# Two blocks on one core: common runs of transposes, and modulation products in 16 runs

## The chip, the cores and the metric

The kernel runs on one core of a Trainium2 chip. The metric is its time on the device in microseconds (us). The core has TensorE (PE; its weight loads are shown as PEld), VectorE (DVE), ScalarE (ACT), GpSimd (POOL) and SyncE (SP), whose queue issues the loads from memory.

## What is computed

Two residual blocks, one behind the other, each of two layers, on 256 tokens of width 1024. A layer of the first block multiplies the tokens by a wide weight matrix, runs three kinds of attention on the parts, gates the result, multiplies by an output matrix and normalizes. A layer of the second block normalizes its 256 tokens and 256 context tokens, scales and shifts them by a modulation that comes from two vectors, multiplies by `w_in`, runs a convolution, a gated linear attention and a softmax attention, merges them under gates, and adds the result, scaled by the modulation's third part:

```python
shift_x, scale_x, gate_x = jnp.split(jax.nn.silu(c) @ w_mod + b_mod, 3, axis=-1)
shift_c, scale_c, gate_c = jnp.split(jax.nn.silu(c_ctx) @ w_mod + b_mod, 3, axis=-1)
hx = rms_norm(xs, norm_g) * (1 + scale_x[:, None]) + shift_x[:, None]
...
xs = xs + gate_x[:, None] * merge(px, ya_x, yb_x, yc_x)
```

All of it is in float32.

## The kernel before

**Weights.** Every product of tokens and weights is made of three matmuls (`mm3`, lines 183 to 186): weights and tokens are each split into a rounded high part (`wh`, made by ScalarE) and a rest (`wl`, made by VectorE). They are called split matmuls here. `WStream` (line 111) holds one table of all weight entries, 512 KB each for the most part, in the order of their use. `_dma` loads the next entry into one of four buffers (`wraw`), `_split` splits it into one of five pairs of buffers (`wh`, `wl`), and `get(key)` first brings loads and splits ahead by so many entries of the table (6 and 3 for most of the kernel) and then hands out the parts of `key`. A `wraw` buffer comes free when its entry is split. All loads go through SP's queue in the table's order.

**Modulation.** `w_mod` is 48 more entries (units) of the same table, 24 for each layer of block 2, in three sets of eight for shift, scale and gate. They are not split. `mod_stream` (line 762) takes one unit, multiplies it with the two vectors (line 770: four products with 32 columns of weights each, side by side in the array, 8 instructions in the trace), and yields; behind the eighth unit of a set it copies the sums, turns them by four small matmuls (line 778) and adds the bias. A unit's `wraw` buffer comes free when its products are done. `FILL` (line 42) says before the use of which weights how many units are taken: 24 places, 24 units in the second layer of block 1, 16 in the first of block 2, 8 in its second. A unit stands in the table just ahead of the weights before which it is used, and counts as an entry of the look-ahead.

**Transposes.** Between the gemms, tokens-by-features results are turned by matmuls with the identity into one of three PSUM banks (`at`) and copied out. In block 1: `gemm` (line 238) calls `post` for each of the two token blocks, and `post_a` and `post_rope` turn the rotated result (lines 292, 271); `gate` (line 576) turns the gated result (line 581) for the output product `go`; `flip` (line 654) turns rows at the end. In block 2: `post_k` (line 928) turns low-rank gates and keys (lines 938, 952), `scores` (line 1022) turns queries and the negated row maxima (lines 1031, 1053), `weigh` (line 1058) turns the attention's output (line 1091), `conv_finish` (line 1330) turns forth and back (lines 1337, 1349), and `norm_prep` (line 791) sums squares by small matmuls (line 815).

**Order.** The program is written in the order of use; a scheduler then lays down each engine's queue ahead of time, taking what is ready by priority (earlier in the program first, unless `high_priority` says otherwise). On the chip each queue runs in the order laid down. `STEPS` gives the order of block 1's steps: gemms A to I, index scores `ix`, attentions `ds`, `df`, `fo`, and gates `h`, `i`, each for token blocks 0 and 1. `g.wait(a, b)` makes instruction a wait for b.

## Time and profile before

| | |
|---|---|
| median of 3 runs | 1189.15 us (1187.99 to 1195.4) |
| the profiled execution's own time | 1192.62 us |
| its span, first to last instruction | 1190.8 us |
| busy: PE, PEld | 1168.5 us, 975.7 us |
| busy: DVE, ACT, POOL | 921.1 us, 569.5 us, 11.2 us |
| mean granted TensorE clock | 0.999 |

The profile is of one execution. Busy time is the time in which an engine had an instruction in work. Matmuls overlap: one starts before the one ahead of it has ended, so the distance from start to start tells more than an instruction's duration.

### The profile page before, as it was taken

How to read it: one execution, taken by the hardware profiler on the slowest of the kernel's cores; microseconds unless marked ns; L12 is line 12 of the kernel's file. 1: busy time of each engine (PE TensorE's matmuls, PEld its weight loads, DVE VectorE, ACT ScalarE, POOL GpSimd, SP SyncE). 2: the span in 40 equal slices, each digit the busy share in tenths (PEclk: the TensorE clock that was granted, in tenths of full speed). 3: DMA queues.
4: the chain of work that ended last, by engine and by line, in shares of the span. 5: the costliest groups of instructions: out<-in, count | busy, mean ns of one | idle time of the engine just before them, and what ended most of it. 6: DMA issues, size and time to landing. Idle time of an engine off the chain costs nothing.

```text
span 1190.8 us, 20632 instructions
## 1 busy us (share of the span) xinstructions
PE 1168.5 (98%) x8024; PEld 975.7 (82%) x8024; DVE 921.1 (77%) x2051; ACT 569.5 (48%) x1024; POOL 11.2 (1%) x42
## 2 busy tenths in 40 slices
PE   8999999999999999999999999999999999999998
PEld 6788777677887777767887888888999778999998
DVE  6996766967799859989545986755799897896984
ACT  5556634456555433247444422433455534855552
POOL 0000000000000000000000000000000000000000
PEclk9999999999999999999999999999999999999999
DMA  7634566465555642024221232325545333554552
GB/s 263 224 125 127 186 207 225 155 229 195 177 194 181 230 137 89 19 73 145 68 84 59 89 100 78 106 89 177 178 142 186 96 107 123 179 162 127 174 176 72
DMA packets 47538, 171.33 MB, mean 144 GB/s; under 512 B 5260, under 2 KB 5900, under 8 KB 46672
## 3 DMA queue, kind: packets, MB, share of 16 engines
q1 hardware_dynamic: 47440, 170.01, 43.7%
q8 instruction: 63, 1.03, 0.3%
q14 instruction: 35, 0.29, 0.1%
HBM read 167.89 MB, written 2.10 MB: 143 GB/s over the span
## 4 chain that ended last, share of the span: by engine, by line
PE 76%; DVE 11%; DMA 6%; ACT 5%; issue 2%; SPq 0%; ACTq 0%; DVEq 0%
PE f0m L186 3%; PE f0m L185 3%; PE f0m L184 3%; PE f1m L186 2%; PE f1m L184 2%; PE f1m L185 2%; PE po L185 1%; PE po L186 1%; PE po L184 1%; PE mod L770 1%; PE go L186 1%; PE go L185 1%; PE go L184 1%; PE yog L186 1%; PE yoc L186 1%
## 5 line engine op out<-in xcount | busy, mean ns | idle before, releaser
L1012 DVE SCALAR_TENSOR_TENSOR ucv<-up,par,ucv 128x512 f32<-128x512 f32 (+1 forms) x240 | 147.3, 614 | 2.8
L184 PE MATMUL f0m<-hTh,wh_0m 128*128 128x512 f32 x192 | 75.1, 391 | 0.0
L185 PE MATMUL f0m<-hTl,wh_0m 128*128 128x512 f32 x192 | 75.1, 391 | 0.0
L186 PE MATMUL f0m<-hTh,wl_0m 128*128 128x512 f32 x192 | 74.8, 390 | 0.0
L184 PE MATMUL f1m<-hTh,wh_1m 128*128 128x256 f32 x192 | 54.9, 286 | 0.1
L186 PE MATMUL f1m<-hTh,wl_1m 128*128 128x256 f32 x192 | 54.8, 286 | 0.0
L185 PE MATMUL f1m<-hTl,wh_1m 128*128 128x256 f32 x192 | 54.5, 284 | 0.0
L154 ACT CAST wh_0m<-wr_0m 128x1024 fp32r<-128x1024 f32 x24 | 25.1, 1047 | 55.9 <-PE f0m L185 14.5
L155 DVE TENSOR_TENSOR wl_0m<-wr_0m,wh_0m 128x1024 fp32r<-128x1024 f32 x24 | 29.3, 1222 | 18.2 <-ACT wh_0m L154 18.1
L184 PEld LDWEIGHTS f0m<-hTh,wh_0m 128*128 128x128 f32 x192 | 36.1, 188 | 7.4
L185 PEld LDWEIGHTS f0m<-hTl,wh_0m 128*128 128x128 f32 x192 | 36.1, 188 | 7.3
L186 PEld LDWEIGHTS f0m<-hTh,wl_0m 128*128 128x128 f32 x192 | 36.1, 188 | 7.3
L184 PEld LDWEIGHTS f1m<-hTh,wh_1m 128*128 128x128 f32 x192 | 36.8, 191 | 0.5 <-ACT wh_1m L154 0.3
L186 PEld LDWEIGHTS f1m<-hTh,wl_1m 128*128 128x128 f32 x192 | 36.7, 191 | 0.2 <-DVE wl_1m L155 0.2
L185 PEld LDWEIGHTS f1m<-hTl,wh_1m 128*128 128x128 f32 x192 | 36.8, 191 | 0.1
L154 ACT CAST wh_1m<-wr_1m 128x1024 fp32r<-128x1024 f32 x24 | 24.9, 1049 | 24.4 <-PE f1m L185 7.6
L155 DVE TENSOR_TENSOR wl_1m<-wr_1m,wh_1m 128x1024 fp32r<-128x1024 f32 x24 | 29.3, 1221 | 8.6 <-ACT wh_1m L154 8.4
L155 DVE TENSOR_TENSOR wl_0o<-wr_0o,wh_0o 128x1024 fp32r<-128x1024 f32 x8 | 9.8, 1224 | 13.2 <-ACT wh_0o L154 13.2
L1413 DVE SCALAR_TENSOR_TENSOR xT<-po,mod,xT 128x256 f32<-128x256 f32 x16 | 7.7, 483 | 14.3 <-PE po L186 14.3
L185 PE MATMUL po<-mgl,wh_0o 128*128 128x256 f32 x64 | 18.2, 285 | 0.0
L186 PE MATMUL pp<-mgh,wl_0p 128*128 128x256 f32 x64 | 18.2, 284 | 0.0
L185 PE MATMUL pp<-mgl,wh_0p 128*128 128x256 f32 x64 | 18.2, 284 | 0.0
(1857 smaller groups left out, 3960.6 us busy)
## 6 DMA issues: line engine op xcount, KB each, us to landing
wr_0mod<-in_wm_dram SPq DMA_DIRECT2D x24, 512.0 KB, 4.5
wr_1mod<-in_wm_dram SPq DMA_DIRECT2D x24, 512.0 KB, 3.7
wr_0m<-in_w_dram SPq DMA_DIRECT2D x24, 512.0 KB, 3.5
wr_1m<-in_w_dram SPq DMA_DIRECT2D x24, 512.0 KB, 3.5
wr_0O<-in_w1o_dram SPq DMA_DIRECT2D x8, 512.0 KB, 3.6
wr_1O<-in_w1o_dram SPq DMA_DIRECT2D x8, 512.0 KB, 3.6
wr_0o<-in_wo_dram SPq DMA_DIRECT2D x8, 512.0 KB, 3.6
wr_0p<-in_wo_dram SPq DMA_DIRECT2D x8, 512.0 KB, 3.7
```

The lines of the kernel that those rows point to most:

```text
L154: g.nc.scalar.copy(wh, r)
L155: g.nc.vector.tensor_sub(wl, r, wh.bitcast(F32))
L184: nc.tensor.matmul(out, lh, rh, start=start, stop=False)
L185: nc.tensor.matmul(out, lh, rl, start=False, stop=False)
L186: nc.tensor.matmul(out, ll, rh, start=False, stop=stop)
L770: nc.tensor.matmul(ps[32 * q:32 * q + 32], g.cz[:, k // 2, 2 * (k % 2):2 * (k % 2) + 32], w[:, 0, 256 * q:256 * q + 256], start=k == 0, st ...
L1012: yield nc.vector.scalar_tensor_tensor(o, src, dw[:, i, j:j + 1], o, op0=OP.mult, op1=OP.add)
L1413: nc.vector.scalar_tensor_tensor(r[:, f, :], ps[:, :256], g.mod[l][:, 16 + f, w:w + 1], r[:, f, :], op0=OP.mult, op1=OP.add)
```

## The change

Modulation: the sets of units are taken in pairs (`MODS`), one unit of each set at a step, both into one PSUM bank; so three pairs of sets instead of six sets. `FILL` becomes a list of 16 places (key, late, steps): eight of one step (2 units), all in the second layer of block 1, and eight of two steps (4 units), all in the first layer of block 2. The products are emitted at `key`, but their entries stand in the table `late` (2 or 3) weight entries further on. The first product of a place waits for the last load of that place, and the products have high priority. `behind` counts the look-ahead in weight entries alone.

Transposes: in each place named above that has two token blocks (or two halves), the vector work of both comes first and the transposes of both follow; the first transpose waits for the vector work of the later one. The attention's output is turned next to the row maxima of the following head group. In block 1 the gate steps of both token blocks become one (`h`, `i`), and in its first layer `h` moves behind gemm I.

The diff, cut to its core:

```diff
-STEPS = ('A B ix0 E C ix1 ds0 ff D ds1 lam df0 F df1 G fo0 fo1 H h0 I h1 i1 i0', 'A B E ix0 ix1 ds0 C ff ds1 lam D df0 df1 F G fo0 fo1 H h0 h1 I i0 i1')
+STEPS = ('A B ix0 E C ix1 ds0 ff D ds1 lam df0 F df1 G fo0 fo1 H I h i', 'A B E ix0 ix1 ds0 C ff ds1 lam D df0 df1 F G fo0 fo1 H h I i')
-FILL = '1B2 2 1E2 3 1D2 3 1F0 2 1G0 2 1H2 1 0Va0 2 0Va1 2 0Va2 2 0GV0 1 0ag0 2 0ag2 2 1GV0 3 1ag0 2 1ag2 2 1A0 1 0BQ2 2 1F2 2 1GK0 1 1B0 1 1A3 5 1C2 1 0ag1 1 1H0 1 0GK0 2'
+FILL = (('1A2', 2, 1), ('1B1', 2, 1), ('1E0', 2, 1), ('1E3', 2, 1), ('1C2', 2, 1), ('1D2', 2, 1), ('1F1', 2, 1), ('1H0', 2, 1), ('0AQ2', 3, 2), ('0BQ2', 3, 2), ('0Va1', 3, 2), ('0Va3', 3, 2), ('0GK1', 3, 2), ('0GV1', 3, 2), ('0ag0', 3, 2), ('0ag3', 3, 2))
+MODS = (((0, 1), (0, 0)), ((0, 2), (1, 1)), ((1, 0), (1, 2)))
...
     def whole(self, key):
         i = self.idx[key]
-        self.ahead(i)
+        while self.nd <= i:
+            self._dma()
         key, src, off, kk, n = self.table[i]
         return self.raw.pop(i).rearrange("p (k n) -> p k n", k=kk)
+    def behind(self, i, n):
+        while n and i < len(self.table) - 1:
+            i += 1
+            n -= self.table[i][0] not in self.f32
+        return i
     def ahead(self, i):
-        while self.nd < min(len(self.table), i + self.ad + 1):
+        while self.nd < min(len(self.table), self.behind(i, self.ad) + 1):
             self._dma()
-        while self.ns < min(len(self.table), i + self.asp + 1):
+        while self.ns < min(len(self.table), self.behind(i, self.asp) + 1):
...
     def get(self, key):
         self.ad, self.asp = self.looks.pop(key, (self.ad, self.asp))
-        for _ in range(self.fills.pop(key, 0)):
-            next(self.stream)
         i = self.idx[key]
+        if key in self.fills:
+            n, last = self.fills.pop(key)
+            while self.nd <= self.idx[last]:
+                self._dma()
+            self.go = self.loads[last]
+            for _ in range(n):
+                next(self.stream)
         self.ahead(i)
         return self.spl[i]
...
+        flips = []
         for tb in range(2):
             part(tb, range(h, nch))
-            post(ps[tb], tb)
+            flips.append(post(ps[tb], tb))
+        if isinstance(flips[0], tuple):
+            for i in range(2):
+                first = flips[i][1]()
+                if i == 0:
+                    g.wait(first, flips[1][0])
...
-        rope(ps, 0, 8, r, tb, f'{nm}{l}{tb}')
-        transp(r.rearrange("p h d -> p (h d)"), 4, dst[:, :, tbs[tb]], f'{nm}{l}{tb}', 0.125 if nm == 'dq' else 1.0)
+        roped = rope(ps, 0, 8, r, tb, f'{nm}{l}{tb}')
+        return roped, lambda: transp(r.rearrange("p h d -> p (h d)"), 4, dst[:, :, tbs[tb]], f'{nm}{l}{tb}',
+                                     0.125 if nm == 'dq' else 1.0)
...
+    def gate(c):
+        for tb in range(2):
+            sg = gates[:, tb, 512 * c:512 * c + 512]
+            done = nc.vector.tensor_mul(sg, sg, mixed[:, tb, 512 * c:512 * c + 512])
+        for tb in range(2):
+            sg = gates[:, tb, 512 * c:512 * c + 512]
+            pt = pp.tile([128, 4, 128], F32, name=f'mt{l}{c}{tb}', tag='at', bufs=g.AT)
+            for i in range(4):
+                t = nc.tensor.transpose(pt[:, i, :], sg[:, 128 * i:128 * i + 128], idf)
+                if tb == 0 and i == 0:
+                    g.wait(t, done)
+            split_out(g, mTh[:, 4 * c:4 * c + 4, tbs[tb]], mTl[:, 4 * c:4 * c + 4, tbs[tb]], pt, 0.5,
+                      sc['g'] if c == 0 else None)
...
-            for c in range(2):
-                pt, ks = flip(mixed[:, tb, :], tb, c)
+            for pt, ks in [flip(mixed[:, tb, :], tb, c) for c in range(2)]:
                 nc.scalar.copy(nxT[:, ks, tbs[tb]], pt)
...
-def mod_stream(g, l, W):
+def mod_stream(g, W):
     nc, sp, pp = g.nc, g.sp, g.pp
-    for s in MORDER:
-        ps = pp.tile([128, 256], F32, name=f'mod{l}{s}', tag='gm', bufs=g.GM)
+    for n, two in enumerate(MODS):
+        ps = pp.tile([128, 512], F32, name=f'mod{n}', tag='gm', bufs=g.GM)
         for k in range(8):
-            w = W.whole(f'{l}mod{s}{k}')
-            for q in range(4):
-                nc.tensor.matmul(ps[32 * q:32 * q + 32], g.cz[:, k // 2, 2 * (k % 2):2 * (k % 2) + 32],
-                                 w[:, 0, 256 * q:256 * q + 256], start=k == 0, stop=k == 7)
+            ws = [W.whole(f'{l}mod{s}{k}') for l, s in two]
+            with g.tc.high_priority():
+                for h in range(2):
+                    for q in range(4):
+                        m = nc.tensor.matmul(ps[32 * q:32 * q + 32, 256 * h:256 * h + 256],
+                                             g.cz[:, k // 2, 2 * (k % 2):2 * (k % 2) + 32],
+                                             ws[h][:, 0, 256 * q:256 * q + 256], start=k == h == 0, stop=k == 7,
+                                             skip_group_check=True)
+                        if h == q == 0 and W.go is not None:
+                            g.wait(m, W.go)
+                            W.go = None
...
+                m = nc.tensor.matmul(ss[:, c:c + 1], pr[:, i, 128 * b:128 * b + 128], g.ones[:, 0:1], start=i == 0, stop=i == 1)
+                if i == b == 0:
+                    g.wait(m, added)
...
+        late = []
         for tb in tbs:
             part(tb, range(h, nch))
-            post(ps[tb][:, :n], tb)
+            late.append(post(ps[tb][:, :n], tb))
+        if isinstance(late[0], tuple):
+            for i, (_, flip) in enumerate(late):
+                first = flip()
+                if i == 0:
+                    g.wait(first, late[1][0])
...
+        done = gain(kb, 2, 1) if tb < 2 else rope2(kb, 2, tb - 2, 1, f'k{tb}')
+        return done, lambda: flip_k(kl, tb)
+
+    def flip_k(kl, tb):
+        kb = kl[:, 0:128]
+        pl = pp.tile([96, 128], F32, name=f'lrt{l}{tb}', tag='at', bufs=g.AT)
+        first = nc.tensor.transpose(pl, kl[:, 128:224], idf)
         pt = pp.tile([128, 128], F32, name=f'akt{l}{tb}', tag='at', bufs=g.AT)
         nc.tensor.transpose(pt, kb, idf)
...
+        def flip(after):
+            pt = pp.tile([128, 2, 128], F32, name=nm + 'ot', tag='at', bufs=g.AT)
+            for i in range(2):
+                t = nc.tensor.transpose(pt[:, i, :], o[:, 128 * i:128 * i + 128], idf)
+                if i == 0 and after is not None:
+                    g.wait(t, after)
+            c = 128 * tb - T0
+            nc.scalar.activation(aoT[:, 2 * kv:2 * kv + 2, c:c + 128], pt, AF.Copy, scale=0.5)
+        yield flip
...
         nxt = scores(tb, kv)
         qs = next(nxt)
+        flip = got = None
         for st in range(4):
-            next(prev, None)
-            next(nxt, None)
+            flip = next(prev, None) or flip
+            got = next(nxt, None) or got
+        if flip is not None:
+            flip(got)
         prev = weigh(tb, kv, *qs)
-    for _ in prev:
+    for flip in prev:
         pass
...
+                t = nc.tensor.transpose(pt[:, 128 * tb:128 * tb + 128], ns[tb][:, 128 * f:128 * f + 128], idf)
+                if f == tb == 0:
+                    g.wait(t, normed)
...
+    fills, at, m = {}, {}, 0
+    for k, late, n in FILL:
+        at[keys[keys.index(k) + late]] = mods[m:m + 2 * n]
+        m += 2 * n
+        fills[k] = n, mods[m - 1][0]
+    assert m == len(mods)
+    tab = []
     for e in seq:
+        tab += at.get(e[0], []) + [e]
```

## Rows read from the trace of the kernel before

**Rows 1.** The page's first part: engine, busy us (share of span) x instructions.

```profile
PE 1168.5 (98%) x8024; PEld 975.7 (82%) x8024; DVE 921.1 (77%) x2051; ACT 569.5 (48%) x1024; POOL 11.2 (1%) x42
```

**Rows 2.** Waits of PE: line <- releaser: us in total, times, longest us.

```profile
PE dft L477 <- DVE dfe L473: 2.4, 4, 1.6
...
PE is L316 <- ACT ir L320: 1.5, 3, 0.8
```

**Rows 3.** Timeline of PE: start us, us, line, out<-in, count; one modulation unit.

```profile
221.04 0.40 PE L186 MATMUL g1C<-wh_1C,xTl 128*128 128x512 f32 x1
221.37 0.64 PE L770 MATMUL mod<-wr_0mod,cz 128*32 128x256 f32 x8
221.94 0.50 PE L184 MATMUL g1C<-wh_1C,xTh 128*128 128x512 f32 x1
222.28 0.40 PE L185 MATMUL g1C<-wl_1C,xTh 128*128 128x512 f32 x1
```

**Rows 4.** The same view, two units in one run.

```profile
381.86 1.07 PE L770 MATMUL mod<-wr_1mod,cz 128*32 128x256 f32 x16
382.86 0.50 PE L184 MATMUL f0Va<-hTh,wh_0Va 128*128 128x512 f32 x1
```

**Rows 5.** The same view, first and last of 34 stretches of line 770.

```profile
161.65 0.63 PE L770 MATMUL mod<-wr_0mod,cz 128*32 128x256 f32 x4
...
1004.65 1.07 PE L770 MATMUL mod<-wr_1mod,cz 128*32 128x256 f32 x16
```

**Rows 6.** Waits of PEld: us in total, times, longest us.

```profile
PEld mod L770 <- issue: 8.3, 27, 0.4
```

**Rows 7.** Timeline of PE, two waits at modulation runs: [idle before <-releaser].

```profile
169.71 0.62 PE L770 MATMUL mod<-wr_0mod,cz 128*32 128x256 f32 x2 [0.66 <-DMA wr_0mod<-in_wm_dram]
...
406.28 0.50 PE L184 MATMUL f0Va<-hTh,wh_0Va 128*128 128x512 f32 x1 [0.85 <-ACT wh_0Va L154]
```

**Rows 8.** Timeline of PE, four transposes in one run and eight in one.

```profile
137.90 0.39 PE L185 MATMUL g0I<-wl_0I,xTh 128*128 128x512 f32 x1
138.13 0.39 PE L186 MATMUL g0I<-wh_0I,xTl 128*128 128x512 f32 x1
138.36 0.60 PE L581 MATMUL mt<-cst,gt 128*128 128x128 f32 x4
138.72 0.48 PE L184 MATMUL go<-wh_0O,mTh 128*128 128x512 f32 x1
139.03 0.39 PE L185 MATMUL go<-wl_0O,mTh 128*128 128x512 f32 x1
...
141.17 0.40 PE L185 MATMUL go<-wl_0O,mTh 128*128 128x512 f32 x1
141.41 1.03 PE L581 MATMUL mt<-cst,gt 128*128 128x128 f32 x8
142.19 0.48 PE L186 MATMUL go<-wh_0O,mTl 128*128 128x512 f32 x1
142.51 0.40 PE L184 MATMUL go<-wh_0O,mTh 128*128 128x512 f32 x1
```

**Rows 9.** Waits of PE (as rows 2), and one such wait in the timeline.

```profile
PE akt L952 <- DVE kb L919: 1.1, 3, 0.5
...
33.30 0.63 PE L271 MATMUL iq00tp<-cst,iq 128*128 128x128 f32 x4 [0.24 <-DVE iq L265]
```

**Rows 10.** Load issues: queue, count, KB each, us from issue to landing.

```profile
wr_1mod<-in_wm_dram SPq DMA_DIRECT2D x24, 512.0 KB, 3.7
```

**Rows 11.** The page's costly groups, splits: count | busy, mean ns | idle before, releaser.

```profile
L154 ACT CAST wh_0m<-wr_0m 128x1024 fp32r<-128x1024 f32 x24 | 25.1, 1047 | 55.9 <-PE f0m L185 14.5
L155 DVE TENSOR_TENSOR wl_0m<-wr_0m,wh_0m 128x1024 fp32r<-128x1024 f32 x24 | 29.3, 1222 | 18.2 <-ACT wh_0m L154 18.1
```

**Rows 12.** Timeline of ACT, the copy behind a gate's transposes.

```profile
139.05 0.68 ACT L219 ACTIVATE mTh<-mt,gsc 128x512 fp32r<-128x512 f32 x1
```

**Rows 13.** Windows: us, busy (x count) by engine, PEclk, DMA share, GB/s; then timeline of PE.

```profile
9.00:16.50 7.50, 6.02 (x20) 5.04 (x21) 5.81 (x8) 5.36 (x8) 0.00 (x0) 0.77 1.02 410
734.00:740.00 6.00, 6.00 (x35) 5.08 (x34) 4.51 (x9) 1.05 (x1) 0.00 (x0) 1.00 0.26 87
...
736.59 1.47 PE L1337 MATMUL cvt<-cst,ucv 128*128 128x128 f32 x12
```

## What the change is expected to do

> **What bounds the kernel now.** I read the page's first part, then TensorE's waits, then stretches of TensorE's timeline around every kind of work that the change moves. TensorE stands at 98% busy, VectorE at 77%, ScalarE at 48% [rows 1]. The 98% alone says little, since a matmul's time overlaps the next one's; so I looked at the steps from start to start. In the timeline a split matmul of 512 columns follows the one before it after 0.23 us [rows 8], layer after layer, and the stretches that keep to such a step fill most of the span. TensorE's waits confirm it: with the first weights' load left aside, the longest sums behind another engine are 2.4 us for the `dft` transposes and 1.5 us for `is` [rows 2]. TensorE's queue is therefore the path. What counts is each step in it that is longer than it need be, and the change aims at two kinds: where modulation products stand between split matmuls, and where transposes do.
>
> **The modulation products.** In the timeline one unit (512 KB of weights, 8 instructions) costs this: the last split matmul starts at 221.04, the products at 221.37, the next split matmul at 221.94 and the one after that at 222.28 [rows 3]; an ordinary step is 0.23 [rows 8]. Two units in one run take 1.00 us from their start to the next split matmul instead of 0.57 [rows 3, 4]. So a unit costs 0.43 us, and a run has a fixed part besides: 0.33 - 0.23 = 0.10 on the way in, 0.57 - 0.43 = 0.14 in the run, 0.34 - 0.23 = 0.11 behind it, together 0.34 us (0.35 by rounding).
>
> How many runs are there? Counting them in the timeline gives 34 unbroken stretches of line 770, the first at 161.65, where half a unit is cut off by transposes, the last at 1004.65 [rows 5]. `FILL` asks for 24 places; others are cut by transposes or attention matmuls that came first. After the change there are 16, eight of two units and eight of four, each held together by one wait and raised in priority. 18 runs fewer at 0.34 is 6.1 us; cut pieces that border on transposes have a somewhat smaller fixed part, so I take **-5.8**. The lower bound: the weight loader sat idle in front of the products 27 times for 8.3 us in all, 0.31 each [rows 6]; 27 - 16 = 11 of these make 3.4 us. The 48 units themselves cost the same before and after.
>
> **Waits beside these products.** Once a run waited 0.66 us for a weight that had to be loaded into a buffer which the run itself was freeing (`1A3`, five units against four buffers), and once 0.85 us went by behind a run, because the splits' look-ahead counted modulation entries as weights and so `0Va2`'s split came late [rows 7]. New runs have at most four units and `behind` no longer counts them: **-1.3**, between 0 and -1.5.
>
> **The merged transposes.** Four transposes in one run: from the split matmul before them to the second one after them 0.90 us; eight: 1.34 us [rows 8]. Less two ordinary steps (0.46) that is 0.44 and 0.88: eight in one run cost what two runs of four cost, to the 0.01 us of the timeline. By the code some 70 groups of transposes and small products become about 30 (`gemm` A to D in two layers 16 to 8, `gate` 8 to 4, keys 16 to some 6, the 12 attention outputs joined to the row maxima's transposes, the rest in `flip`, `norm_prep` and `conv_finish`); some stand together already, like the eight of [rows 8], so that some 35 go. At 0 to 0.02 each: **-0.2**, between 0 and -0.7. The Trainium skill (TensorE: Matmul & The Clock Gate, Single matmul latency) gives an isolated matmul a fixed part of 398 cycles at 2.4 GHz, 0.17 us, which it cannot hide; by an estimate from it, with a switch in and a switch out, 35 merges would bring 12 us. The timeline shows none of that for transposes, and the measurement decides.
>
> What merging does change is waiting. TensorE takes its queue in order, so a transpose whose vector work is late holds up the matmuls behind it: `akt` waited 1.1 us in three places, `iq00tp` 0.24 [rows 9]. A merged run waits once, for the later half; half of these 1.3 us is **-0.7**, between 0 and -1.3. On the other side, behind each such run stands the gemm that fills the time, and behind that its evictions; see the rivals.
>
> **What is added.** Each run waits for its last load. Before, products stood at their place in the program with slack (one wait on a load in 34 runs); now they are ready exactly when the last load lands, since they are emitted two or three weights ahead and have priority. If the load is later on the chip than the order assumes, TensorE stands, and the split matmuls queue behind it. Between 0 and 16 x 0.66 = 10.6 us; nearer to the trace's one in 34, I take two such waits, **+1.3**.
>
> Four units fill all four `wraw` buffers, so SP's queue can't load the next weight until the run has begun. That weight then needs 3.7 us to land [rows 10] and 1.05 + 1.22 us to split [rows 11], 6.0 us. Covered elsewhere by three split weights, each 24 matmuls x 0.23 = 5.5 us. At `0AQ2` the cover is thin: three of five `wh` buffers hold the keys' weights, and a `BQ` weight feeds one token block for 6 x 0.23 = 1.4 us only. One wait like that of `Va2`: **+0.9**, between 0 and 2 x 0.85.
>
> In layer 0 of block 1 `gate` for the first half moves behind gemm I. Its transposes, then 0.68 us of ScalarE [rows 12] stand before the first `go` matmul. Gemm I covers it if the run falls within I, as one of them does now; without cover one ScalarE copy is bare. **+0.4**, between 0 and 0.7. The moved loads (16 units in block 1's second layer instead of 24, 32 in block 2's first instead of 16, none in its second instead of 8) change TensorE's work in no stage but by these units. The wider copy and sums behind the products run on ScalarE and VectorE while split matmuls go on: nothing.
>
> **The sum** is -5.8 - 1.3 - 0.2 - 0.7 + 1.3 + 0.9 + 0.4 = -5.4 us. The profiled execution took 1192.62 us (span 1190.8), 3.47 above the median of 1189.15. On its own time that is 1187.2, against the median **1183.7 us**. Waits that no edit names (`dft`, `is`, 3.9 us together) may go or double when the queue's order is made anew: 1179.8 to 1187.6 is this case's own range.
>
> **Rivals.**
>
> *Runs that wait for their last load (slower).* Place: the first product of each run. For it: the one wait on a load in the trace was in a run placed at its load's landing. Against it: the other 33 had none. At 0.66 us in all 16 runs, 10.6 replaces 1.3: +3.9, 1193.0 us. It decides from 0.42 us a run on ((5.4 + 1.3) / 16).
>
> *Chains behind merged runs (slower).* Thirty merged runs each stand 0.24 us, like `iq00tp`, behind the later half's vector work: 7.2 in place of -0.7 gives +2.5, 1191.6 us. For it: VectorE is busy 77% and its queue is in order too. Against: the gemm that follows fills most such places now.
>
> *All terms at their good bound.* -6.1 - 1.5 - 0.7 - 1.3 with nothing added is -9.6: 1179.5 us. With the unnamed 3.9 gone too, 1175.6.
>
> *The runs don't stay whole.* If each is cut once, as pieces were before, 16 x 0.34 = 5.4 comes back: 1189.1 us, no change. Against: all products of a run become ready at one landing and have priority.
>
> *The clock.* Common runs could lower TensorE's clock. At the start, around TensorE's wait for its first weights, the granted clock over 9 to 16.5 us was 0.77, one part at 1.2 GHz and the rest at 2.4. But 12 transposes in one run at 736.59 stood in a stretch with a granted clock of 1.00 [rows 13]. If eight matmuls behind each of 30 merged runs went at 1.2 GHz and took twice their 0.23 us, that is 55 us more: 1239 us. The Trainium skill says so on its own (TensorE: Matmul & The Clock Gate, PE-mode transpose): transposes don't count as TensorE activity for the clock gate. By that rule longer runs of them work against the change; this trace shows no drop behind the longest.
>
> **How the numbers follow.** Chances: the sum 0.61, waits on the last load 0.12, chains 0.10, all good bounds 0.10, cut runs 0.05, the clock 0.02. The likeliest gives 1183.7. The range runs from 1175 (all good, unnamed waits gone) to 1196 (waits on loads, with most of another 3.9); outside it lie the upper part of the waits, the clock and tails, under 0.2. A measurement tells about 1% from no change, 11.9 us. Faster than 1177.3: part of the good bounds and a tail of the sum, 0.13. Slower than 1201: longer waits on loads or chains than the rows show, and the clock, 0.09. Between: 0.78.
>
> **What would show it.** Right: 16 stretches of modulation products of 16 and 32 instructions, the weight loader's idle time in front of them falling from 8.3 to some 5 us, the step behind a merged run 0.32 then 0.23 as now, no product of a modulation run waiting for a load. Wrong: a row of TensorE with idle time released by a `wr_0mod` or `wr_1mod` load in several runs; idle time in front of line 271's, the keys' or the attention outputs' transposes larger than now; a wait for `wh_0BQ` or `wl_0BQ`; the first `go` matmul of block 1's layer 0 waiting for `mTh`; a granted clock under 1.00 past 20 us. If the 48 units were not 0.43 us each in the longer runs, the first term is wrong; if transposes after the change take less than 0.11 us each in a run of eight or more, the third is.

## Result and profile after

The changed kernel takes 1199.14 us (median; 1196.55 to 1203.53), the kernel before, run beside it, 1191.92 us (1187.99 to 1196.25). The ratio is 1.0064, with a 95% interval of 1.0049 to 1.0079: slower by 7 us, where the prediction said 5.4 us faster. The profiled execution is the slowest one, 1203.53 us with a span of 1201.8, so its waits are somewhat longer than those of a usual execution.

The page of the changed kernel, busy time of each engine and the granted clock in 40 slices:

```profile
PE 1165.8 (97%) x8024; PEld 982.3 (82%) x8024; DVE 920.5 (77%) x2051; ACT 569.1 (47%) x1021; POOL 11.1 (1%) x42
...
PEclk9999999999998999999999999999999999999999
```

Busy time hardly tells the two kernels apart [rows 1]. The waits of TensorE do (line <- releaser: us in total, times, longest):

```profile
PE mod L806 <- DMA wr_1mod<-in_wm_dram: 12.4, 4, 8.1
PE mod L806 <- DMA wr_0mod<-in_wm_dram: 5.1, 5, 1.4
...
PE dft L502 <- DVE dfe L498: 0.9, 3, 0.4
...
PE is L341 <- ACT ir L345: 0.7, 2, 0.4
...
PE go L197 <- ACT mTh L232: 0.4, 1, 0.4
```

Before, products waited for a load once, 0.66 us [rows 7]. Now TensorE stands 17.5 us in front of nine runs of products. The waits for `dft` and `is` are smaller than before [rows 2]. The 16 runs are whole, eight of two units and eight of four, as the change means them to be.

**Where on the time line.** I cut both traces at the first split matmul of a gemm: `1A` (block 1, layer 1), `0AQ` and `0Va` (block 2, layer 0), `1Va` (block 2, layer 1). The column in the middle counts what moved: a unit at 0.43 us, a run at 0.34, both from [rows 3, 4], and a split matmul at 0.23 [rows 8].

| stretch | before | after | by what moved | measured |
|---|---|---|---|---|
| `1A` to `0AQ` | 184.9 | 180.4 | -7 units, -7 runs: -5.3 | -4.5 |
| `0AQ` to `0Va` | 34.1 | 49.1 | +4 units, +10 `BQ` matmuls: +4.0 | **+15.1** |
| `0Va` to `1Va` | 518.2 | 522.1 | +12 units, -4 runs, -10 `BQ` matmuls: +1.5 | +3.9 |
| `1Va` to the last matmul | 285.8 | 280.6 | -8 units, -5 runs: -5.1 | -5.2 |

The ten matmuls are the rest of gemm `BQ`. Before, they stood behind the first two matmuls of `Va`; in the changed kernel, and in every experiment but the first, all 48 of `BQ` stand ahead of `Va`. The kernel before:

```profile
382.86 0.50 PE L184 MATMUL f0Va<-hTh,wh_0Va 128*128 128x512 f32 x1
383.20 0.40 PE L185 MATMUL f0Va<-hTl,wh_0Va 128*128 128x512 f32 x1
383.43 0.40 PE L185 MATMUL t0BQ<-wl_0BQ,hTh 128*128 128x512 f32 x1
...
385.51 0.39 PE L186 MATMUL t0BQ<-wh_0BQ,hTl 128*128 128x512 f32 x1
```

The last stretch is where the count puts it; `1A` to `0AQ` is 0.8 us above the count and `0Va` to `1Va` 2.4 us. By far the most, 11.1 us, is lost in the one stretch of 34 us. Its window before and after (us, busy time and count of PE, PEld, DVE, ACT and POOL, granted clock, DMA share, GB/s):

```profile
348.79:382.86 34.07, 33.41 (x206) 26.17 (x204) 33.16 (x136) 22.00 (x43) 0.00 (x0) 1.00 0.46 161
```

```profile
345.88:395.01 49.13, 39.60 (x250) 30.48 (x249) 46.52 (x191) 25.99 (x53) 0.00 (x0) 0.93 0.56 193
```

**What stands in it.** SP's queue of the changed kernel, issues only:

```profile
345.54 0.33 SPq L130 DMA_DIRECT2D wr_0mod<-in_wm_dram  x1
351.26 0.33 SPq L130 DMA_DIRECT2D wr_1mod<-in_wm_dram  x1
354.15 0.33 SPq L130 DMA_DIRECT2D wr_0mod<-in_wm_dram  x1
362.34 0.33 SPq L1839 DMA_DIRECT2D xsp<-xres  x1
365.84 0.33 SPq L130 DMA_DIRECT2D wr_1mod<-in_wm_dram  x1
370.77 2.04 SPq L130 DMA_DIRECT2D wr_0BQ<-in_w_dram  x3
```

And TensorE's timeline (start, us, line, out<-in, count, in brackets idle time before and its end):

```profile
360.91 0.66 PE L689 MATMUL yt<-cst,mx 128*128 128x128 f32 x4 [0.17 <-ACT xres L724]
369.64 1.08 PE L806 MATMUL mod<-wr_0mod,cz 128*32 128x256 f32 x8 [8.07 <-DMA wr_1mod<-in_wm_dram]
370.46 1.11 PE L806 MATMUL mod<-wr_1mod,cz 128*32 128x256 f32 x8
...
373.54 0.38 PE L197 MATMUL t0AKV<-wh_0AKV,hTh 128*128 128x288 f32 x1
```

The split of `BQ0` and SP's wait for it (in the last line: us in total, times, longest):

```profile
362.36 1.10 ACT L154 CAST wh_0BQ<-wr_0BQ 128x1024 fp32r<-128x1024 f32 x1
...
364.53 1.23 DVE L155 TENSOR_TENSOR wl_0BQ<-wr_0BQ,wh_0BQ 128x1024 fp32r<-128x1024 f32 x1 [0.27 <-issue]
...
SPq L130 <- DVE wl_0BQ L155: 3.0, 1, 3.0
```

The run keyed `0AQ2` needs four loads. With `BQ0` and the first three of them all four raw buffers are taken, and `BQ0` holds its buffer until VectorE has split it, at 365.76. SP's queue, past the spill of `xres` to memory (`xsp`), waits 3.0 us for this; the fourth load is issued at 365.84, and the run starts 3.8 us later. TensorE has stood since 361.57: 4.2 us until the buffer is free, 3.8 for the load. The key's gemm stands behind the run for as long.

**The clock behind the waits.** Three stretches past the start have a granted clock of 0.50, that is 1.2 GHz; the profiled execution of the kernel before has none:

```profile
216.30:219.70 3.40, 3.40 (x9) 2.57 (x9) 3.12 (x14) 0.00 (x0) 0.00 (x0) 0.50 0.31 124
366.50:373.30 6.80, 3.66 (x33) 1.67 (x34) 6.80 (x41) 1.26 (x2) 0.00 (x0) 0.50 0.46 137
...
410.90:414.30 3.40, 3.40 (x18) 2.11 (x11) 0.00 (x0) 0.18 (x1) 0.00 (x0) 0.50 0.89 283
```

The first comes behind runs that waited 1.2, 0.8 and 1.4 us, the second in and behind the 8.07 us, the third behind a wait of 2.6 us. In them every step is longer than the same step elsewhere; summed over the matmuls that start there it is 1.6 + 1.8 + 1.4 = 4.8 us. In the second stretch four units take 3.0 us from first to last product, and 1.56 at the full clock (experiment 4).

**The sum of the two spans**, 1201.8 - 1190.8 = 11.0 us: waits for loads +16.9 (17.5 - 0.7), clock +4.8, all other waits -3.1 (13.3 against 16.4); that makes 18.6, so the steps themselves have become 7.6 us shorter. The saving that the change promised is there. It is paid for twice over.

### The profile page after: what moved, and what is told of

It reads as the page before. It is cut to its first block, busy times and chain, and to the rows that moved or that the text cites. A ratio compares the mean times of both kernels' runs of the same rounds, so it can differ in the third digit from the quotient of the medians.

```text
span 1201.8 us, 20648 instructions
## 1 busy us (share of the span) xinstructions
PE 1165.8 (97%) x8024; PEld 982.3 (82%) x8024; DVE 920.5 (77%) x2051; ACT 569.1 (47%) x1021; POOL 11.1 (1%) x42
## 4 chain that ended last, share of the span: by engine, by line
PE 77%; DVE 10%; DMA 6%; ACT 4%; issue 2%; SPq 0%; ACTq 0%; DVEq 0%
PE f0m L198 3%; PE f0m L199 3%; PE f0m L197 3%; PE mod L806 2%; PE f1m L197 2%; PE f1m L198 2%; PE f1m L199 2%; DMA wr_1mod<-in_wm_dram 2%; PE po L198 1%; PE po L199 1%; PE po L197 1%; PE go L197 1%; PE go L198 1%; PE go L199 1%; DMA wr_0mod<-in_wm_dram 1%
## 5 line engine op out<-in xcount | busy, mean ns | idle before, releaser
L806 PE MATMUL mod<-wr_0mod,cz 128*32 128x256 f32 x192 | 14.6, 405 | 17.2 <-DMA wr_1mod<-in_wm_dram 11.9
L806 PEld LDWEIGHTS mod<-wr_0mod,cz 128*32 128x32 f32 x192 | 5.6, 113 | 23.1 <-issue 15.0
```

The lines of the kernel that those rows point to most:

```text
L806: m = nc.tensor.matmul(ps[32 * q:32 * q + 32, 256 * h:256 * h + 256], g.cz[:, k // 2, 2 * (k % 2):2 * (k % 2) + 32], ws[h][:, 0, 256 * q:2 ...
```

## Experiments

Two questions: which part of the change costs the time, and whether it is the place of a run in the queue (theory W at first), the merged transposes (T) or the long runs as such (S). Ratios are to the kernel before on the same chip, with 95% intervals. What is read from a trace is that of one execution.

**1 and 2: one part alone.** The kernel before with the new transposes and the old products, and the other way round.

> The kernel before with the merged transposes, the later gate and the waits between them; modulation products, their loads and the look-ahead stand as before (34 stretches). Theory W (the products' place): the changed kernel loses its time only where runs of products stand in TensorE's queue at the moment their last load is expected, 17.5 us of waits on wr_0mod and wr_1mod in its trace; the transposes gain. From its trace, the steps into transposes sum to 68.4 us against 71.2 before, so W expects 2 to 4 us below the kernel before (about 1189). Rival T (chains behind merged transposes): merging costs time through the wait for the later half; it expects 2 to 7 us above the kernel before (1194 to 1199).

> The kernel before with the new modulation products alone: 16 runs, pairs of units, loads two or three weights ahead, one wait and raised priority, and the look-ahead that skips modulation entries; all transposes as before. Theory W: 18 runs fewer save about 6 us of fixed parts, and about 17 us of waits on the last load are added: 9 to 12 us above the kernel before (1201 to 1204), with 16 unbroken stretches and over 12 us of TensorE's idle time released by wr_0mod and wr_1mod. Rival T: about 6 us below the kernel before (1186). Rival S (long runs cost by themselves, through the clock behind them): above the kernel before, but with little idle time released by loads and stretches at a granted clock of 0.5 behind the runs.

Transposes alone: 1192.98 us, 0.9999 (0.9988 to 1.0009), no stretch at 0.5 past the start. They neither gain nor lose; W's 2 to 4 us and T both fail. Products alone: 1198.62 us, 1.0046 (1.0027 to 1.0065): the loss is theirs, at 2 us under the range of W. But the waits were not the expected ones:

```profile
PE akt L976 <- DVE qn00v L208: 6.0, 1, 6.0
PE mod L787 <- DMA wr_1mod<-in_wm_dram: 3.2, 3, 1.9
...
PE mod L787 <- DMA wr_0mod<-in_wm_dram: 1.6, 3, 0.6
```

Only 4.8 us on loads. At the same place as the 8.07 us, TensorE now stands 6.0 us for vector work on the keys, and a stretch at 0.5 begins at 361.5 and lasts 10.2 us. From `0AQ` to `0Va` it takes 49.8 us, much as the changed kernel does. One stretch, two different waits: the first sign that the wait's name isn't the cause.

**3 and 4: the place of the runs, and the loads of one.**

```diff
-    nc.tensor.matmul(out, ll, rh, start=False, stop=stop)
+    mm3.last = nc.tensor.matmul(out, ll, rh, start=False, stop=stop)
...
                             g.wait(m, W.go)
+                            g.after(m, mm3.last)
```

```diff
-('0AQ2', 3, 2)
+('0AQ2', 2, 2)
```

> The changed kernel, whose runs may not stand in TensorE's queue before the split matmul that the program emits ahead of them; whole runs, loads and waits as they are. In the queue a run moves back by 4 to 73 split matmuls of 0.23 us in 14 of 16 places; the run keyed 0AQ2 (8.07 us of waiting) and that keyed 0BQ2 stay where they are. Theory W: the 9.4 us of waits of the other runs shrink to under 2, the 8.1 us at 0AQ2 stay: 7 to 9 us below the changed kernel, 1190 to 1192, level with the kernel before. Rival S (long runs cost by themselves): no change against the changed kernel, 1199. A third way, that a later run holds back the load of the next weight through the raw buffers: the waits move to wh_ and wl_ of the weights behind, and 1195 to 1199.

> The changed kernel with one edit: the four loads of the run keyed 0AQ2 stand one weight earlier in the load order (ahead of BQ0, not of BQ1), so that none stands behind the spill of xres on SP's queue and none needs the buffer that BQ0's split frees. Theory W: the 8.1 us wait in front of that run goes, and the 1.4 us that its products lost in a stretch with a granted clock of 0.5: 8 to 9.5 us below the changed kernel, 1190 to 1191. Rival: BQ0 now loads behind the run, and TensorE waits for wh_0BQ instead: 3.7 us of load and 2.3 us of splits less what the keys' gemm covers, so 2 to 6 us come back and the gain is 2 to 7 us. Rival S (long runs cost by themselves): within 1 us of the changed kernel.

The place alone: 1197.73 us, 1.0044 (1.0028 to 1.0059). What is left of the waits for loads:

```profile
PE mod L806 <- DMA wr_1mod<-in_wm_dram: 11.8, 3, 7.4
```

In block 1 all of them are gone, and `1A` to `0AQ` falls to 175.7 us. How the raised place makes them is seen at one run. In the changed kernel its last load is issued at 244.18 and it stands in the middle of gemm D:

```profile
247.15 0.39 PE L197 MATMUL g1D<-wh_1D,xTh 128*128 128x512 f32 x1
248.92 1.07 PE L806 MATMUL mod<-wr_0mod,cz 128*32 128x256 f32 x16 [1.38 <-DMA wr_0mod<-in_wm_dram]
```

Here it stands behind D, starts at 249.83 and waits for nothing. Yet the gain in the medians is 1.4 us, not 7 to 9. 7.4 us at `0AQ2` stay, as W had said; 3.3 us are left at `0Va1`; and the stretch at 0.5 behind the first has become 10.2 us. (Between the two profiled executions the gain is 6.2 us, but that of the changed kernel is its slowest.) One run's loads earlier: 1193.53 us, 1.0010 (0.9997 to 1.0023), 5.6 us below the changed kernel, though the 8.07 us wait is 0.22 now. The rest has come back further on: the second run stands behind the first matmul of `Va`, and 1.9 us go for `wh_0Vb`, with a stretch at 0.5 at 392.1; `0AQ` to `0Va` is 36.0 us, and `0Va` to the first matmul of `GK` 6.8 us longer than before, with six units more (2.6 us) in it. W's number fails; the rival's gain of 2 to 7 us holds, with another weight than it named.

**5 to 8: both edits together, and taken apart.** The place, and the loads of all eight runs of block 2 one weight earlier (`3, 2` to `2, 2`); the same on the kernel with old transposes; the loads alone; and both with `0AQ2` put back.

> The changed kernel with both edits: runs no earlier in TensorE's queue than the split matmul that the program emits ahead of them, and the loads of all eight runs of block 2 one weight earlier in the load order. What the first four experiments left standing: with the place alone, 11.8 us of waits on three loads (7.4 at 0AQ2, 3.3 at 0Va1, 1.2 at 0BQ2) and 4.0 us lost in one stretch with a granted clock of 0.5 behind the first. Theory W (waits and the clock behind them are the whole loss; the products' fixed part gains 6 us, the transposes 0 to 3): under 2 us of waits on loads, no stretch at 0.5 past 20 us, 5 to 8 us below the kernel before, 1184 to 1187. Rival N (a wait moves on to the weight that stands behind a run in the load order, as wh_0Vb did with 1.9 us when one run was loaded earlier): 2 to 4 us of waits on wh_ or wl_, often with a stretch at 0.5, 1188 to 1191. Rival S (long runs lower the clock by themselves): stretches at 0.5 behind runs that did not wait, 1192 or more.

> The same two edits on the kernel with the new products alone; all transposes as in the kernel before. Theory W with the gain in the products: 16 runs for 34 at 0.34 us each are 5.8 us, so 1185 to 1188, and no more than 1 or 2 us above the run with the merged transposes. Rival (the merged transposes carry the gain once the waits are gone): 1190 to 1192, 4 or more above it.

> The changed kernel with the loads of all eight runs of block 2 one weight earlier, and the runs' raised place as in the changed kernel (in the queue they move forward again with their loads, by up to 29 split matmuls). Theory W, by which the raised place sets the wait (a run stands where its last load is expected, wherever that load is): 5 to 8 us of waits on wr_0mod and wr_1mod in many small pieces, with the 8 us wait at 0AQ2 gone, 1190 to 1194. Rival L (the load order alone sets the wait): under 2 us of them in block 2, 1185 to 1188.

> The kernel with both edits, in which the loads of the run keyed 0AQ2 alone stand where the changed kernel has them (behind BQ0). It prices that one wait with all that follows it. Theory W: 7 to 8 us of waiting in front of that run and 3 to 4 us lost in a stretch at a granted clock of 0.5, together 10 to 12 us above the kernel with both edits. Rival: TensorE would have stood there for the keys' vector work in any case (as for 6.0 us at the keys' transposes with the products alone), so that the load's part is small: 2 to 5 us above the kernel with both edits.

Both edits: 1195.10 us, 1.0020 (1.0010 to 1.0030), where W wanted 1184 to 1187. The waits for loads are 1.6 us in all, but look at TensorE between `BQ` and `Va`:

```profile
376.70 0.50 PE L198 MATMUL t0BQ<-wl_0BQ,hTh 128*128 128x512 f32 x1 [0.96 <-DVE wl_0BQ L155]
380.51 0.64 PE L806 MATMUL mod<-wr_0mod,cz 128*32 128x256 f32 x8 [1.25 <-DMA wr_1mod<-in_wm_dram]
...
384.64 0.29 PE L1001 MATMUL lrt<-cst,kb 128*96 128x128 f32 x1 [2.20 <-DVE kb L972]
...
388.03 0.79 PE L197 MATMUL f0Va<-hTh,wh_0Va 128*128 128x512 f32 x1 [1.78 <-ACT wh_0Va L154]
```

A split, a load, vector work, a split: 6 us in four pieces, and a stretch at 0.5 from 387.7 on for 6.8 us. The stretch takes 46.0 us. With old transposes 1194.58 us (1.0028, 1.0013 to 1.0044) and 46.0 us there; the loads alone 1198.02 us (1.0044) and 47.1 us; with `0AQ2` put back 1194.89 us (1.0016, 1.0004 to 1.0028) and 49.0 us there, the wait at `0AQ2` being 7.6 us again. So putting back the longest wait costs nothing, where W wanted 10 to 12 us and its rival 2 to 5: theory W in its first form is finished. On experiment 6 both texts fail. Rival N's kind of wait came true, at a price above its range. The loads alone leave 7.3 us of small waits, as W said of the raised place, but stay 4 us above its range. What all kernels with both runs ahead of `Va` share is a stretch of 46 to 50 us in place of 34, whichever wait stands in it (the text on experiment 9 says "every kernel"; experiment 4, with one of the runs behind `Va`, is the exception).

**9 to 12: theory K, that this stretch cannot take eight units.** In it stand the two runs keyed `0AQ2` and `0BQ2`, eight units; before there were four. The edit moves them to where block 2's first layer has long gemms:

```diff
-('0AQ2', 3, 2), ('0BQ2', 3, 2), ('0Va1', 3, 2), ...
+('0Va1', 2, 2), ..., ('0ag3', 2, 2), ('0m3_2', 2, 2), ('0gg0', 2, 2)
```

> The kernel with both edits (place in the program, loads of block 2 one weight earlier), in which the two runs keyed 0AQ2 and 0BQ2 go to 0m3_2 and 0gg0, later in block 2's first layer. So far, from the first split matmul of AQ to the first of Va every kernel with these two runs takes 46 to 49 us (changed kernel 49.1, both edits 45.9, products alone with both edits 46.0) against 34.1 before, whichever wait stands there, while block 1's second layer and block 2's second layer gain 7.1 and 5.0 us. Theory K (that stretch cannot load and split eight more half-megabyte units beside its own weights; the wait only changes its name): without them it falls to 32 to 34 us, no stretch at a granted clock of 0.5 past 20 us, and the kernel is 6 to 9 us below the kernel before, 1183 to 1186. Rival P (a run of four units costs as much at its new places, by loads or by the buffer it holds): the 8 to 10 us come back behind the first f0m matmul, 1192 to 1195.

> The changed kernel with one edit: the two runs keyed 0AQ2 and 0BQ2 go to 0m3_2 and 0gg0 (loads three weights ahead, raised place, as all its runs). Theory K: the stretch from AQ to Va falls from 49.1 us to 32 to 34, and of the changed kernel's loss only the small waits of the other runs stay, 5 to 9 us: 12 to 14 us below the changed kernel less the two runs' own 3.7, that is 1187 to 1191. Rival (the raised place is the main cause): waits of over 3 us at the new places or at Va1, 1194 to 1199.

> The first kernel of this set without its edit of the place: two runs moved, loads of block 2 one weight earlier, raised place as in the changed kernel. It prices the raised place where nothing else is wrong. Theory W: 4 to 7 us of waits on loads in block 1 and a stretch or two at 0.5 behind them (1.5 us each), so 5 to 8 us above the first kernel of this set, 1189 to 1193. Rival: the raised place costs under 2 us.

> The kernel before with nothing of the change, but with eight units between AQ and Va (four at 0AQ2, four at 0BQ2; before: two at 0BQ2 and two at 0Va0), six taken from 0Va0 to 0Va2. Its units load directly ahead of their key, without the common wait and without raised place. Theory K: the stretch from AQ to Va becomes longer by 8 to 12 us of which the four more units are 1.7, the stretches behind it shorter by 2 to 3: 1197 to 1202. Rival F (the form of the runs, their wait and place make the loss there): at most 2 us more in the stretch, 1191 to 1194.

All three edits: **1182.79 us, 0.9914 (0.9895 to 0.9932)**, below both kernels. No product waits for a load, and the stretch is back at its length, with no unit in it and the ten `BQ` matmuls more. One point of K's text fails: a stretch at 0.5 of 3.4 us at 225.3, behind a wait of 1.8 us for vector work.

```profile
341.40:374.63 33.23, 33.12 (x182) 27.44 (x181) 32.20 (x124) 24.29 (x44) 0.00 (x0) 1.00 0.47 163
```

The old products with eight units in the stretch, six of them taken from `0Va0` to `0Va2` behind it, and nothing else changed: 1195.32 us, 1.0021 (1.0005 to 1.0037), and

```profile
348.84:393.01 44.17, 40.02 (x250) 29.36 (x248) 42.49 (x173) 25.82 (x51) 0.00 (x0) 1.00 0.62 213
```

10.1 us more than before, where the four additional units are 1.7 and the ten `BQ` matmuls 2.3. So the stretch becomes longer without the new form of the runs. But that isn't the loss: `0Va` to `1Va` gave back 6.5 us instead of 2 to 3, and the total is 2 us under K's range and 1 us above rival F's. From `0AQ` to `1Va`, with the same 16 units, this kernel is 3.6 us longer than the kernel before; the changed kernel is 19.0 us longer there, of which its 16 more units and four fewer runs are 5.5. So eight units in the stretch cost some 3 us in the old form, and the changed kernel loses 13.5 on the same way, 4.5 of them in waits of later runs and at 1.2 GHz behind these. K holds for the length of the stretch; for the loss, the form of the runs counts as well.

Moving the two runs alone: 1191.31 us, 0.9989 (0.9973 to 1.0005), with 33.5 us in the stretch and 6.9 us of small waits left, 0.3 us above K's range; its executions spread over 9 us, and the profiled one is the fastest. With earlier loads but the raised place: 1193.39 us, 1.0011 (0.9995 to 1.0027), and

```profile
PE mod L806 <- DMA wr_1mod<-in_wm_dram: 6.2, 5, 2.6
PE mod L806 <- DMA wr_0mod<-in_wm_dram: 5.7, 5, 1.9
```

against none when the runs stand at their place in the program. That prices the raised place, with nothing else wrong, at 10.6 us, more than W's 5 to 8.

**13 to 15: the square, the transposes again, and the loads.**

> The changed kernel with the edit of the place and the two runs moved to 0m3_2 and 0gg0; loads three weights ahead as in the changed kernel. It closes the square of two edits: neither 1199.1, place alone 1197.7, moved alone 1191.3. If the two causes add, 1190; theory K (a wait gained in block 1 is lost again in the stretch from AQ to Va while the two runs stand there, so that each edit shows fully only with the other): within 2 us of the kernel with all three edits, 1181 to 1185. If instead the earlier loads were what mattered with all three edits: 1189 to 1192.

> The kernel with the new products alone (transposes as before) with all three edits: place, earlier loads in block 2, two runs moved. It prices the merged transposes where no run waits. If the transposes bring nothing, as beside the old products (1193.0 against 1192.3): within 2 us of the kernel with all three edits, 1181 to 1185. If they bring what the steps into transposes showed in the changed kernel (2.8 us): 1185 to 1187. If the merged transposes only pay once no run waits: 1187 to 1190.

> The changed kernel, in which the two runs keyed 0AQ2 and 0BQ2 load nothing: their 64 products read the high half of a weight already in SBUF (the weight ahead of their key) and the 8 loads are left out, 4 MB; so half of one modulation vector is not that of the reference. Runs, places and everything else as in the changed kernel. Theory K as a matter of loads (four raw buffers, SP's queue and the splits behind them): the stretch from AQ to Va takes 34 to 37 us instead of 49.1 though TensorE does the same products there, 1185 to 1190 in all. Rival V (VectorE's work on the keys, or the products themselves, set that stretch): 42 us or more, 1194 or more.

| | runs raised | runs at program place |
|---|---|---|
| `0AQ2`, `0BQ2` where they were | 1199.14 (1.0064) | 1197.73 (1.0044) |
| moved to `0m3_2`, `0gg0` | 1191.31 (0.9989) | 1182.96 (0.9916) |

Place and moved runs alone give 0.9916 (0.9897 to 0.9934), so the earlier loads weren't needed. The two edits don't add: 1.4 and 7.8 alone, 16.2 together. Why they don't stays open. The profiled executions don't show it: by them the place gives 6.2 us in the upper row and 2.7 in the lower, since the one of the changed kernel is its slowest and the one of experiment 10 its fastest. Part of the spread goes with the clock: in experiment 10 the four executions at a mean granted clock of 1.000 take 1186.1 to 1189.9 us, the slowest, 1195.16, has 0.995; in experiment 13 all lie between 0.997 and 1.000.

Old transposes with all three edits: 1181.27 us, 0.9909 (0.9891 to 0.9927), within the intervals the same as with the new ones. The merged transposes bring nothing in any setting.

The changed kernel without the two runs' eight loads: 1188.88 us, 0.9969 (0.9955 to 0.9984), and

```profile
344.79:384.17 39.38, 37.79 (x247) 29.34 (x245) 38.18 (x148) 24.80 (x45) 0.00 (x0) 1.00 0.42 140
```

Of the 15.1 us, 9.8 go with the loads, 1.7 are the products of four more units, 2.3 the ten `BQ` matmuls, and 1.3 remain, of which 1.2 is a wait for `wh_0AQ`. The stretch is 2 us longer than K wanted, and the total is in its range. So the loads are most of the cause. But leaving them out also changed what the scheduler laid down: the two runs, with no load to be ready for, start at 346.48 and 366.14 instead of 369.64 and 388.76, so their places are not as they were.

Which part of the loads' way is the narrow one is seen at one load only, the fourth of `0AQ2`: a raw buffer, and behind it a split. It isn't the DMA engines: their share in the stretch is 0.56 in the changed kernel, against 1.02 at the start [rows 13]. VectorE can't be excluded. It is busy for 95% of the stretch, as it was for 97% before, but it does 13.4 us more there (46.5 us against 33.2), mostly work on keys and queries that stood behind the first `Va` before; without the loads it does 38.2. Whether this work sets the length of the stretch or only fills it, no run parts; a fifth raw buffer wasn't tried either.

## Why the prediction was wrong

**Fixed part of a run, -5.8: right, and too small.** From the last matmul ahead of a run to the second behind it, start to start, less two ordinary steps, the 34 stretches before take 34.5 us in sum, the 16 runs of experiment 9 25.0. These 9.5 contain the 0.66 and 0.85 us of [rows 7], for which I had put -1.3; the fixed part itself gave 8.0 us. Less 0.43 us for each of 48 units, one of the 34 cost 0.36 us on the average and one of the 16 costs 0.27, where I had 0.34 for both; pieces cut by transposes were no cheaper, against what I had thought.

**Waits on the last load, +1.3: the step that failed first.** It measured 17.5 us in the profiled execution. I took the rate of the trace of before, one run in 34, although those products stood at their place in the program. The prediction names the difference itself ("now they are ready exactly when the last load lands") and then uses the old rate. The upper end, 16 times 0.66 us, was no bound either, because the longest wait seen is no bound for a wait of another kind: one alone was 8.07. The rival built on it had the right sign and a chance of 0.12; at 1193.0 us it was 6 us short.

**"No stage but by these units": the step that cost most.** The term said that moved loads change TensorE's work in no stage but by the units' own time. It holds to 0.1 us from `1Va` on, where units only went. `1A` to `0AQ` is 0.8 us above the count, with 5.1 us of waits in front of runs there; experiment 3, without these waits, is 3.9 us below it. From `0AQ` to `0Va` the term fails by 13.4 us: 2.3 are the `BQ` matmuls, since the new loads changed the order laid down as well, and 11.1 are lost time. I had even worked out, under the full raw buffers, that "at `0AQ2` the cover is thin", and priced it at one wait of 0.85 us for a `BQ` weight. The place was right. What was late was the run's own fourth load, and when that was cured, a split, vector work on the keys and `wh_0Va` in turn. The question to ask was not which wait comes, but how many loads, in runs of four, the stretch takes in 34 us: it has four weights of `BQ` that feed only 12 matmuls each (I had counted 6), a spill and, after the change, eight units instead of four. With the loads of these two runs gone, or the runs moved, the 11 us went; by what part of their way stays open.

**The clock, at 0.02: right effect, wrong trigger.** I tied it to merged transposes. It follows standing still: each kernel with a wait of 6.0 us or more at `0AQ2` (the changed one, and experiments 2, 3 and 8) has a stretch at 1.2 GHz of 6.8 to 10.2 us there, for load and vector work alike; experiment 4 runs the same four units at the same key behind a wait of 0.22 us in 1.56 us at a clock of 1.00. At the start TensorE had waited for its first weights when the clock was low [rows 13], so the row to see it was on the list. The Trainium skill (TensorE: Matmul & The Clock Gate, Loop structure matters more than you think) warns that matmuls behind a long wait on a transfer run cold; the trace agrees, with 1.8 us lost so behind the 8.07 us in the changed kernel. Of its rule on transposes (PE-mode transpose), which I weighed instead, no run here shows an effect: the profiled executions of experiments 1 and 13, with all merged runs, have no stretch at 0.5 between the start and 1182 us.

**Transposes, -0.2 and -0.7: right within the measurement** (0.9999, and no difference in experiments 6 and 14). The 12 us by the isolated latency are excluded. **The later gate, +0.4: right**; `go` waits once, 0.39 us for `mTh` at 140.41, in block 1's layer 0. **`dft` and `is`**, 3.9 us before, are 1.6 now: they went, as one side of the range had it.

## What to carry to other kernels

A saving per instruction is added up over the whole kernel, but a load is paid for in the stretch where it is put: before work is moved, count for that stretch how many buffers' worth its own weights need and what covers them, and how many buffers one run of the moved work holds at once. An instruction laid in an in-order queue at the moment its data are expected waits for every delay of the transfer, and all that stands behind it waits too; leave it at a place with slack. And when a cured wait comes back under another name at the same place, measure the length of the stretch and not the wait; then check that the same work lies between its ends, and what the next stretch gives back.

## What the runs showed of the hardware

A wait of TensorE can cost more than its length: 6.0 to 8.1 us of standing brought 6.8 to 10.2 us at 1.2 GHz, with 1.8 to 2.9 us more of matmul time (1.8 in the changed kernel, 2.8 in experiments 3 and 8, 2.9 in experiment 2; the 4.0 and the 3 to 4 in the texts on experiments 5 and 8 were too high). It didn't always take a long wait: the stretch at 216.3 in the changed kernel came behind three of 0.8 to 1.4 us, those in experiments 9, 12 and 14 behind a single one of 1.6 to 1.8 us. Nor did a wait of this size always bring one: the kernel before stood 1.6 us for `dft` [rows 2], and past the start its clock never fell in that execution. Runs of 16 and 32 small products had no effect on the clock by themselves: the profiled execution of experiment 13 has all 16 of them, and no stretch at 0.5 between the start and 1182 us.
